# Branch B first and finished beside the gates, which go branch by branch and are summed in DRAM: one encoder layer on one Trainium2 core

## The chip, the core and the metric

The kernel runs on one core of one Trainium2 chip. A core has a matrix engine (TensorE, PE), a vector engine (VectorE, DVE), a scalar engine (ScalarE, ACT), a general engine (GpSimd, POOL) and SyncE (SP), which here only starts transfers. The metric is the device time of one execution in microseconds (us). Before the change it is 1698.8 us, the median of three runs (1694.76, 1698.8 and 1701.2).

## What is computed

One layer of a hybrid encoder on 1024 prompt tokens and 32 sample tokens, with a model width of 1024, five branches of width 256, and a feed-forward block. All of it is in float32:

```python
xn = rmsnorm(x, norm1_g)
z = xn @ w_in
ga = jax.nn.gelu(za)
va = layernorm(ga[..., W:], a_ln_g, a_ln_b)
oa = ua * gmlp_spatial(va, a_ws, a_bs)
b_in = zb[..., :W] * jax.nn.sigmoid(zb[..., W:])
b_ext = jnp.concatenate([hist_b, b_in], axis=1)
ob = jax.nn.silu(layernorm(causal_dwconv(b_ext, b_conv_w) + b_conv_b, b_ln_g, b_ln_b))
c_ext = jnp.concatenate([hist_c, c_c * c_x], axis=1)
oc = c_b * causal_dwconv(c_ext, c_conv_w)
od = multiscale_pool(d_ext, pos0, d_w, d_scale)
oe = memory_attention(zq, mem_k, mem_v)
branches = (oa, ob, oc, od, oe)
...
    merged = merged + jax.nn.sigmoid(xn @ w_gate[n] + b_gate[n]) * (branches[n] @ w_branch[n])
x = x + merged @ w_out
x = x + (jax.nn.silu(hn @ w_ffn_gate) * (hn @ w_ffn_up)) @ w_ffn_down
```

`z` is cut into two parts for A, two for B, three for C, one for D and one, the query, for E. Convolution B has 31 taps, C has 3. The states of B, C and D, the memory's keys and values, and the normalised rows of A are outputs too.

## The kernel before

Channels lie on the 128 partitions and tokens along the free axis. The 1056 tokens are two halves (`c` = 0, 1) of 528 columns, each of two quarters of 264 (256 prompt and 8 sample tokens). Each float32 factor is split in a high and a low part (`split`, L141: a copy on ACT, L148, and a subtraction on DVE, L149), and a product takes three passes (`product`, L166). A projection `z` is 128 output channels of one half: 8 input blocks x 3 passes x 2 quarters, 48 matmuls. Its result lies in a pair of PSUM banks. There are two such pairs and four single banks in the first pool of PSUM (`ps1`). When attention is done, `banks.close()` ends it, and a second one with two single banks and three pairs (`ps2`) begins.

Work is put in program order by hand. A `runner` holds a generator, and calling it with a number runs that many of its yields, so that pieces of attention (`att_bg`), of convolution B (`b_bg`) or of the rescaling of the tokens (`again`) stand between two products. Each engine then executes its own instructions in the order in which they stand, and waits where an input is not there.

The order is: memory keys and values; the query `q`; branch C on `xn`, which is x times the norm's weight, with the row factors `r1` and their squares applied behind the product (`x_factor`, `x_spread`); the tokens loaded again and multiplied by `r1`, which gives `xs` (`rescale`); branch B on `xs`, with attention two steps to a projection; D's projection with attention and convolution B beside it; A's projections `ua` and `va` with Gelu, and the rest of convolution B; then the branch products (`branch`) in the order E, C, A, D, B, with D's pooling alone in front of its product. Each product of 128 channels and one half takes 12 matmuls, is copied by ACT (`pb`, L1012) and written to DRAM by a DMA that POOL issues (`pb_d`, L1013).

Convolution B (`conv_b`, L726 to L737) is 60 multiply-and-add instructions (L733) and two plain ones over all 1086 columns of `b_ext` into a second buffer `b_y`, followed by the norm in four pieces (`norm_b`).

The gates are 20 steps, `steps = [(p, n) for p in range(KT // 2) for n in BRANCHES]`, each a pair of output blocks of one branch, computed by seven products of half size (`ORDER`: a11, a12, s2, s1, s3, s4, a22), 24 matmuls a unit. DVE and ACT make the sums and splits of the weights (L1090, L1148, L149) and gather the results (L1179 to L1199). `merge` (L1159 to L1169) takes the sigmoid, multiplies by the branch product (`pin`) and adds to `acc`, which stays in SBUF over the five branches of a pair and is then written to `mg_d`. `load_pair` brings the raw weights of the next step, two tiles, into three buffers.

## Time and profile before

| what | value |
|---|---|
| median of three runs | 1698.8 us |
| the profiled execution | 1698.78 us |
| its span, first to last instruction | 1696.9 us |
| granted clock of PE, mean | 0.987 |
| ACT busy, POOL busy | 686.9 us, 109.6 us |

The profiled execution is the median one, and 1.9 us lie outside its span. Busy times say how much of the span an engine worked. The windows divide the span, and give for each stretch the busy time of every engine beside the clock that PE was granted (1.00 is full speed, 2.4 GHz). A timeline's row is a run of like instructions, and the bracket at its end tells how long the engine sat idle before it, and what ended that. Groups by line give the mean duration of one instruction.

### The profile page before, as it was taken

The page shows a single profiled execution, that of the slowest core. Times are in us where ns is not written, and L with a number is a line of the kernel's source. Part 1 is how long each engine was busy: PE and PEld are TensorE (multiplying, and loading weights), DVE is VectorE, ACT ScalarE, POOL GpSimd, SP SyncE. Part 2 cuts the span into 40 slices and gives each one's busy share as a digit, 9 for nine tenths or more (in the row PEclk, how much of TensorE's full clock was granted, in tenths as well). Part 3 has the DMA queues.
Part 4 walks back from the last instruction along what each step waited for, and adds up shares of the span by engine and source line. Part 5 has one row for each costly group of instructions (what it writes and reads, how often), then busy time and mean ns, then how long its engine had stood idle before and what let it go on. Part 6 is the DMA issues. An engine that isn't in the chain of part 4 may idle for free.

```text
span 1696.9 us, 31557 instructions
## 1 busy us (share of the span) xinstructions
PE 1647.5 (97%) x13248; PEld 1623.0 (96%) x13248; DVE 1107.6 (65%) x1900; ACT 686.9 (40%) x1273; POOL 109.6 (6%) x217
## 2 busy tenths in 40 slices
PE   9999979899999999999999999999999999999997
PEld 8998959889999999999999999999999999999997
DVE  7678998774566677676666786666666666242345
ACT  6325752575544444444452343333333334131221
POOL 0020000223300000000000000000000003000000
PEclk9999979999999999999999999999999999999999
DMA  8252100446723334234362112222222228231012
GB/s 296 84 182 75 39 14 26 156 153 233 277 76 102 127 102 156 86 103 140 120 263 86 64 64 77 87 77 76 76 76 76 76 89 330 101 115 47 29 38 103
DMA packets 59647, 190.87 MB, mean 112 GB/s; under 512 B 9168, under 2 KB 12816, under 8 KB 59504
## 3 DMA queue, kind: packets, MB, share of 16 engines
q1 hardware_dynamic: 35328, 112.75, 20.7%
q0 software_dynamic: 20624, 73.72, 11.7%
q10 hardware_dynamic: 3552, 2.37, 0.4%
...
## 4 chain that ended last, share of the span: by engine, by line
PE 85%; DVE 5%; issue 4%; DMA 2%; ACT 2%; POOL 2%; SPq 0%; POOLq 0%; DVEq 0%; ACTq 0%
PE sa L166 28%; PE sy L166 14%; PE dn L166 13%; PE z L166 7%; PE sx L166 7%; PE wo L166 5%; PE pb L166 2%; PE dq L166 2%; PE va L166 2%; DVE b_y L733 1%; POOL pb_d L1013 1%; PE fs L320 1%; PE ov L166 1%; PE fu L166 1%; DMA pb_d<-pb 1%
## 5 line engine op out<-in xcount | busy, mean ns | idle before, releaser
L166 PE MATMUL sa<-x,s 128*128 128x264 f32 x1968 | 252.6, 284 | 0.0
L166 PEld LDWEIGHTS sa<-x,s 128*128 128x128 f32 x1968 | 244.9, 188 | 0.0
L166 PE MATMUL dn<-hp,hl 128*128 128x264 f32 x1824 | 222.2, 284 | 0.0
L166 PEld LDWEIGHTS dn<-hp,hl 128*128 128x128 f32 x1824 | 222.1, 188 | 0.1
L149 DVE TENSOR_TENSOR s<-s,s 128x512 fp32r<-128x512 f32 x164 | 112.9, 689 | 89.1 <-ACT s L148 88.1
L148 ACT ACTIVATE hl<-raw 128x512 fp32r<-128x512 f32 (+1 forms) x132 | 79.3, 616 | 214.6 <-PE dn L166 125.1
L148 ACT ACTIVATE s<-s 128x512 fp32r<-128x512 f32 x164 | 103.3, 631 | 153.4 <-PE sa L166 77.6
L149 DVE TENSOR_TENSOR hl<-raw,hl 128x512 fp32r<-128x512 f32 (+1 forms) x132 | 87.2, 673 | 89.1 <-ACT hl L148 88.8
L166 PE MATMUL sy<-x,s 128*128 128x264 f32 x984 | 126.2, 284 | 0.0
L166 PE MATMUL sa<-t,a 128*128 128x264 f32 x984 | 125.9, 284 | 0.0
L166 PEld LDWEIGHTS sy<-x,s 128*128 128x128 f32 x984 | 122.2, 188 | 0.0
L166 PEld LDWEIGHTS sa<-t,a 128*128 128x128 f32 x984 | 122.0, 188 | 0.0
L149 DVE TENSOR_TENSOR a<-fr,a 128x512 fp32r<-128x512 f32 x123 | 85.0, 691 | 52.7 <-ACT a L148 52.5
L166 PE MATMUL z<-xs,hl 128*128 128x264 f32 x768 | 99.2, 289 | 9.4 <-DVE oc L687 3.5
L148 ACT ACTIVATE a<-fr 128x512 fp32r<-128x512 f32 x123 | 78.0, 634 | 72.8 <-issue 67.0
L166 PEld LDWEIGHTS z<-xs,hl 128*128 128x128 f32 x768 | 97.1, 193 | 10.6 <-issue 5.7
L166 PE MATMUL z<-xn,hl 128*128 128x264 f32 x768 | 94.4, 284 | 1.8 <-ACT r L378 1.8
L166 PEld LDWEIGHTS z<-xn,hl 128*128 128x128 f32 x768 | 93.5, 188 | 2.3 <-ACT r L378 2.1
L166 PE MATMUL wo<-mg,hl 128*128 128x264 f32 x768 | 94.2, 284 | 0.0
L166 PEld LDWEIGHTS wo<-mg,hl 128*128 128x128 f32 x768 | 93.4, 188 | 0.2
L166 PE MATMUL pb<-br,hl 128*128 128x264 f32 x576 | 76.8, 294 | 6.3 <-ACT br L148 5.0
L1421 DVE TENSOR_TENSOR y<-y,dn 128x528 f32<-128x528 f32 x40 | 28.0, 703 | 82.4 <-PE dn L166 82.4
...
## 6 DMA issues: line engine op xcount, KB each, us to landing
pb_d<-pb POOLq DMA_DIRECT2D x80, 264.0 KB, 2.8
...
```

What stands on the lines that cost most here:

```text
L148: nc.scalar.activation(hl[:, 0], src, AF.Copy)
L149: nc.vector.tensor_tensor(hl[:, 1], src, hl[:, 0].bitcast(F32), op=ALU.subtract)
L166: nc.tensor.matmul(out, w(wi), rhs, start=start and i == 0, stop=stop and i == n - 1, skip_group_check=not (start and stop),)
L320: nc.tensor.matmul(ps[:, q, t0 : t0 + n], ones[: rows[i]], diag[: rows[i], q * Q + t0 : q * Q + t0 + n], start=True, stop=True,)
L733: nc.vector.scalar_tensor_tensor(b_y[:, j, :LB], b_ext[:, j, k : k + LB], col("bw", 31 * j + k), b_y[:, j, :LB], op0=ALU.mult, op1=ALU.add,)
L1013: nc.gpsimd.dma_start(pb_d[n][mt][:, c], out)
L1421: nc.vector.tensor_tensor(quarters(dst), quarters(dst), ps, op=ALU.subtract)
```

## The change

Branch B comes first, on `xn`. The squares of x are put beside the query's products, with the factors of the first half (`x_factor`, `x_spread`) between the last of them. B's projections are multiplied by `r1` behind PSUM, and `xs` is made beside them. C follows on `xs`, with its first tap on ACT. Attention now runs one step to a projection, from C to the last tile of A's `va`. D's projection comes behind A, after the change of PSUM pools.

Convolution B is done per channel half and in pieces of 512, 512 and 32 columns: the first tap on ACT, 30 on DVE, of which the last writes back into `b_ext`. It begins beside `ua` and goes on beside everything that follows, the first 16 gate steps included (`b_bg(2.5)` before each unit). There its norm is finished too, and branch 1's own products (`own_b`) are computed, in single banks and with weights in sixteen small tiles.

The gates go branch by branch, four pairs each. The first branch writes its gated product to `mg_d` by a plain DMA, the next three add to it with accumulating DMAs on POOL's queue, and the last one loads the sum (`acc`) and adds on DVE. The raw weights have two buffers in place of three, asked for behind the last use, and the merge buffers `ft` three in place of four. The FFN shares both.

```diff
-    epool = stage.enter_context(tc.tile_pool(name="epool", bufs=3))
+    epool = stage.enter_context(tc.tile_pool(name="epool", bufs=2))
...
-    for i in (16, 17, 10, 12, 11, 13, 8, 9, 6, 4, 7, 5, 14, 15, 0, 1):
+    for i in (16, 17, 6, 4, 7, 5, 10, 12, 11, 13, 8, 9, 0, 1):
         want("w_in", i)
     for i in (0, 1):
         want("w_va", i)
-    for n in BRANCHES:
+    for i in (14, 15):
+        want("w_in", i)
+    for n in BRANCHES[:-1]:
...
-        spreads[c] = factors([r1[c]], D, late=True)[1]
+        spreads[c] = factors([r1[c]], D, late=True, narrow=True)[1]
 
     def x_spread(c):
-        ps = spreads[c]()
-        nc.scalar.activation(quarters(r1q[c]), ps, AF.Square)
-        nc.scalar.copy(quarters(r1[c]), ps)
+        for q_, ps in enumerate(spreads[c]()):
+            nc.scalar.copy(r1[c][:, q_ * Q : q_ * Q + Q], ps[:, :Q])
...
+    for c in range(NC):
+        x_squares(c)
...
+            if c == 1:
+                (x_factor, x_spread)[j](0)
...
+    again = runner(rescale(0), rescale(1))
     for j in range(2):
         wb_ = [wview(slab()) for _ in range(2)]
         for c in range(NC):
-            ps = projected(wb_[0], c, xs)
-            if j == 0 and c == 0:
-                again(2)
-            elif j:
-                att_bg(2)
+            ps = projected(wb_[0], c, xn)
+            if j == c == 0:
+                x_factor(1)
+            else:
+                again()
             sb = temp(f"sb{j}_{c}")
-            nc.scalar.activation(quarters(sb), ps, AF.Sigmoid)
-            ps = projected(wb_[1], c, xs)
-            if j == 0 and c == 0:
-                again(2)
+            nc.vector.tensor_tensor(quarters(sb), ps, quarters(r1[c]), op=ALU.mult)
+            nc.scalar.activation(sb, sb, AF.Sigmoid)
+            ps = projected(wb_[1], c, xn)
+            if j == c == 0:
+                x_spread(1)
             else:
-                att_bg(2)
+                again()
+            nc.vector.tensor_tensor(sb, sb, r1[c], op=ALU.mult)
...
-        b_y = epool.tile([P, 2, EXT], F32, name="b_y", tag="ext")
         for j in range(2):
-            nc.vector.tensor_scalar(
-                b_y[:, j, :LB], b_ext[:, j, 0:LB], col("bw", 31 * j), col("bb", j), op0=ALU.mult, op1=ALU.add
-            )
-            yield
-            for k in range(1, 31):
-                nc.vector.scalar_tensor_tensor(
-                    b_y[:, j, :LB], b_ext[:, j, k : k + LB], col("bw", 31 * j + k), b_y[:, j, :LB],
-                    op0=ALU.mult, op1=ALU.add,
+            for t0, n in ((0, SEQ // 2), (SEQ // 2, SEQ // 2), (HB + SEQ, DEC)):
+                y = temp("by")[:, :n]
+
+                def tap(k):
+                    return b_ext[:, j, t0 + k : t0 + k + n]
+
+                nc.scalar.activation(
+                    y, tap(HB), AF.Identity, bias=col("bb", j), scale=col("bw", 31 * j + HB)
                 )
-                yield 0.33
-        for c in range(NC):
-            br[1][c] = [unit(F32R, f"ob{c}_{j}") for j in range(2)]
-        normed = [norm_b(b_y, i) for i in range(4)]
-        for t in range(3 * 4 + 6):
-            for i in range(4):
-                if 3 * i <= t:
-                    next(normed[i], None)
-            yield
-
-    def norm_b(b_y, i):
-        lo = i * QP
-        w = QP if i < 3 else LB - lo
-        ys = [b_y[:, j, lo : lo + w] for j in range(2)]
-        both = temp("bsm")
-        sm = both[:, :w]
+                for k in range(HB - 1, -1, -1):
+                    dst = tap(0) if k == 0 else y
+                    nc.vector.scalar_tensor_tensor(
+                        dst, tap(k), col("bw", 31 * j + k), y, op0=ALU.mult, op1=ALU.add
+                    )
+                    yield 0.7 if n > DEC else 0.1
...
+            nc.scalar.activation(y, tap(0), AF.Copy, scale=col("cw", 3 * j))
...
+                ps = projected(wc_[i], c, xs)
+                if j == c == 0:
+                    again()
+                else:
+                    att_bg()
+                evac(j, c, ps)
...
+    def own_b(c):
+        for mt in range(KT):
+            raw = fpool.tile([P, 2, P], F32, name=f"wr{c}_{mt}", tag="wr", bufs=1)
+            nc.sync.dma_start(
+                raw, a["w_branch"][2 + mt // 4].rearrange("p (k n) -> p k n", k=2)[:, :, mt % 4 * P : (mt % 4 + 1) * P]
+            )
+            w = fpool.tile([P, 2, 2, P], F32R, name=f"wp{c}_{mt}", tag="wp", bufs=2)
+            split(w, raw)
+            out = temp("pb")
             yield
-
-    b_bg = runner(conv_b())
-
+            for q_ in range(2):
+                cols = slice(q_ * Q, q_ * Q + Q)
+                ps = bank("pb")[:, :Q]
+                product(
+                    ps, [(lambda i, k=k: w[:, i, k], lambda i, k=k: br[1][c][k][:, i, cols]) for k in range(2)]
+                )
+                nc.scalar.copy(out[:, cols], ps)
+                if q_ == 1:
+                    nc.gpsimd.dma_start(pb_d[1][mt][:, c], out)
+                yield 2
+        br[1][c] = None
+
+    def whole_b():
+        yield from conv_b()
+        yield from norm_b(None)
+        for c in range(NC):
+            yield from norm_b(c)
+            yield from own_b(c)
+
+    b_bg = runner(whole_b())
...
+        project(ua_evac, xs, lambda: (att_bg(), b_bg(2)))
+        att_bg()
+        b_bg(0.7)
...
-    d_bg = runner(pool_mix())
-    d_bg.drain()
-    to_parts(3)
-    branch(3, rest((comb, 0.5)))
-    branch(1, rest((comb, 0.5)))
+    pool_bg = runner(pool_d())
+
+    def beside_c(i):
+        if i == 4:
+            to_parts(0)
+        pool_bg()
+        b_bg(0.4)
+
+    branch(2, beside_c)
+    pool_bg.drain()
+    mix_bg = runner(mix_d())
+
+    def beside_a(i):
+        if i % 2 == 1 and i < 8:
+            mix_bg()
+        elif i == 8:
+            mix_bg.drain()
+            to_parts(3)
+        elif i > 8:
+            comb(0.5)
+        if i > 3:
+            b_bg(0.4)
+
+    branch(0, beside_a)
+    branch(3, lambda i: (comb(0.5), b_bg(0.4)))
...
-            if n_raw[0] % 3 == 2:
-                r = fpool.tile([P, 1024], F32, name=f"fr{p}", tag="fraw", bufs=1)
-            else:
-                r = wpool.tile([P, 1024], F32, name=f"fr{p}", tag="raw", bufs=2)
-            n_raw[0] += 1
+            r = wpool.tile([P, 1024], F32, name=f"fr{p}", tag="raw", bufs=2)
...
-                if n == "s3":
+                if n == ORDER[-1][0]:
                     load_pair(pairs, fraws, p + 1)
...
-    steps = [(p, n) for p in range(KT // 2) for n in BRANCHES]
+    steps = [(p, n) for n in BRANCHES for p in range(KT // 2)]
...
+        pin[n, mt] = unit(F32, f"pi{mt}_{n}")
+        nc.sync.dma_start(pin[n, mt], pb_d[n][mt])
+        if n == BRANCHES[-1]:
+            acc[mt] = unit(F32, f"acc{mt}")
+            nc.gpsimd.dma_start(acc[mt], mg_d[mt])
...
+            nc.vector.tensor_tensor(g, g, pin[n, mt][:, c], op=ALU.mult)
             if n == BRANCHES[0]:
-                nc.vector.tensor_tensor(acc[mt][:, c], acc[mt][:, c], g, op=ALU.mult)
-                return
-            nc.vector.tensor_tensor(g, g, pin[n, mt][:, c], op=ALU.mult)
-            nc.vector.tensor_tensor(acc[mt][:, c], acc[mt][:, c], g, op=ALU.add)
+                nc.gpsimd.dma_start(mg_d[mt][:, c], g)
+            elif n != BRANCHES[-1]:
+                nc.gpsimd.dma_start(mg_d[mt][:, c], g, accum_op=ALU.add)
+            else:
+                nc.vector.tensor_tensor(acc[mt][:, c], acc[mt][:, c], g, op=ALU.add)
...
+        if i < 4 * KT // 2:
+            hooks = {m: lambda: b_bg(2.5) for m, _ in ORDER}
+        if i == 4 * KT // 2 - 1:
+            b_bg.drain()
```

Line numbers shift: `split` is L149 and L150 in the new kernel, convolution B's taps L674, the sums of weights L1100, the gates' gathering L1200 to L1210, `merge`'s multiplication L1174, A's Gelu L808 and L841, attention's exponential L524, its scaling L529 and its transposed copies L546.

First place: ACT in the stretch of the query's products, from the last split of `xn` on (`hl` are split weights, `sq` and `r` squares of x, `q` the copies out of PSUM). Before:

```order
L148 ACTIVATE hl_0_300<-raw_136 128x512
L148 ACTIVATE hl_1_301<-raw_136 128x512
L363 ACTIVATE sq_522<-x_1_128 128x528
L363 ACTIVATE sq_525<-x_1_128 128x528
L363 ACTIVATE sq_528<-x_2_132 128x528
L430 COPY q_298<-z 128x528
L148 ACTIVATE hl_0_310<-raw_306 128x512
L148 ACTIVATE hl_1_311<-raw_306 128x512
L430 COPY q_298<-z 128x528
```

and now:

```order
L369 ACTIVATE sq_304<-x_1_131 128x528
L369 ACTIVATE sq_307<-x_1_131 128x528
L369 ACTIVATE sq_310<-x_2_135 128x528
L149 ACTIVATE hl_0_346<-raw_139 128x512
L149 ACTIVATE hl_1_347<-raw_139 128x512
L365 ACTIVATE r_234<-x_0_129 128x528
L365 ACTIVATE r_234<-x_0_259 128x528
L149 ACTIVATE hl_0_356<-raw_352 128x512
L149 ACTIVATE hl_1_357<-raw_352 128x512
L437 COPY q_344<-z 128x528
```

The first copy of `q` stood ahead of the split of the third weight (`raw_306`) and now stands behind it, and behind three squares and two that start the row sums.

Second place: ACT beside A's `va` tiles (`va` the Gelu, `pe` attention's exponentials and scalings, `pt` its transposed copies). Before:

```order
L148 ACTIVATE hl_1_3017<-raw_2750 128x512
L884 ACTIVATE ua_2742<-z 128x528
L148 ACTIVATE hl_0_3024<-raw_2867 128x512
L884 ACTIVATE ua_2743<-z 128x528
L148 ACTIVATE hl_1_3025<-raw_2867 128x512
L917 ACTIVATE va_3011<-va 128x256 x4
L917 ACTIVATE va_3012<-va 128x256 x4
```

and now:

```order
L841 ACT_TABLE_LOAD
L841 ACTIVATE va_all<-va 128x256
L546 ACTIVATE pt_2456<-tp 128x2x128
L524 ACT_TABLE_LOAD
L524 ACTIVATE pe,sm<-sc,mx 128x256
L546 ACTIVATE pt_2458<-tp 128x2x128
L524 ACTIVATE pe,sm<-sc,mx 128x256
L841 ACT_TABLE_LOAD
L841 ACTIVATE va_all<-va 128x256
L529 ACTIVATE pe<-pe,sm 128x256 x2
```

Eight Gelus stood together, without attention; now each stands between exponentials, with a table load on either side.

Third place: DVE in a gate step (`s`, `a` sums and low parts of weights, `p` and `u` results, `pi` the branch products or the sum; `by` and `b_ext` convolution B). Before, from the first gathering of a step on:

```order
L1189 TENSOR_TENSOR p_7_6820<-sx,p_7_6820 128x528
L149 TENSOR_TENSOR a_8_6884<-fr_6784,a_8_6884 128x512
L1168 TENSOR_TENSOR p_7_6820<-p_7_6820,pi_0_6777 128x528
L1169 TENSOR_TENSOR pi_4_6320<-pi_4_6320,p_7_6820 128x528
L149 TENSOR_TENSOR a_8_6912<-fr_6784,a_8_6912 128x512
L149 TENSOR_TENSOR s_8_6945<-s_8_6943,s_8_6945 128x512
L1194 TENSOR_TENSOR p_7_6819<-sa,p_7_6819 128x528
L149 TENSOR_TENSOR s_8_6976<-s_8_6941,s_8_6976 128x512
L1090 TENSOR_TENSOR s_8_7053<-s_8_6943,fr_6784 128x512
L1168 TENSOR_TENSOR p_7_6819<-p_7_6819,pi_0_6816 128x528
L1169 TENSOR_TENSOR pi_4_6360<-pi_4_6360,p_7_6819 128x528
```

and now, in step 1:

```order
L1200 TENSOR_TENSOR p_1_5051<-sx,p_1_5051 128x528
L150 TENSOR_TENSOR s_1_5056<-s_1_5054,s_1_5056 128x512
L674 SCALAR_TENSOR_TENSOR by<-b_ext,vec,by 128x512
L150 TENSOR_TENSOR a_1_5088<-fr_4836,a_1_5088 128x512
L674 SCALAR_TENSOR_TENSOR by<-b_ext,vec,by 128x512
L1174 TENSOR_TENSOR p_1_5051<-p_1_5051,pi_4_5003 128x528
L674 SCALAR_TENSOR_TENSOR by<-b_ext,vec,by 128x512
L150 TENSOR_TENSOR a_2_5126<-fr_5091,a_2_5126 128x512
L674 SCALAR_TENSOR_TENSOR by<-b_ext,vec,by 128x512
L150 TENSOR_TENSOR a_2_5158<-fr_5091,a_2_5158 128x512
```

The additions to the sum (L1169) are gone from there, and a tap of 512 columns stands behind nearly every instruction. Between the first gatherings of steps 0 and 3 stand 44 wide and 30 narrow taps.

## Rows read from the trace of the kernel before

**Rows 1.** The head of the page and its busy times by engine (share, instructions).

```profile
span 1696.9 us, 31557 instructions
PE 1647.5 (97%) x13248; PEld 1623.0 (96%) x13248; DVE 1107.6 (65%) x1900; ACT 686.9 (40%) x1273; POOL 109.6 (6%) x217
```

**Rows 2.** The table by windows: start:end, length, busy us of each engine (instructions), granted clock, DMA.

```profile
75.00:450.00 375.00, 340.31 (x2569) 322.20 (x2568) 288.20 (x543) 196.71 (x444) 60.01 (x113) 0.95 0.35 117
225.00:250.00 25.00, 15.55 (x66) 9.47 (x67) 21.44 (x41) 12.23 (x39) 0.00 (x0) 0.57 0.00 0
325.00:350.00 25.00, 19.61 (x141) 18.88 (x140) 14.77 (x47) 18.96 (x33) 5.14 (x12) 0.86 0.36 130
350.00:375.00 25.00, 21.86 (x157) 20.91 (x158) 20.74 (x54) 20.59 (x45) 6.58 (x13) 0.93 0.36 134
450.00:863.00 413.00, 413.00 (x3414) 413.00 (x3413) 284.56 (x430) 185.18 (x301) 9.61 (x18) 1.00 0.39 126
```

**Rows 3.** PE's timeline at two holes: start, length, instruction, idle before and releaser.

```profile
227.26 1.11 PE L530 MATMUL tp<-ident,pe 128*128 128x128 f32 x4 [3.52 <-ACT pe L523]
...
337.11 1.40 PE L166 MATMUL pb<-br,hl 128*128 128x264 f32 x3 [4.99 <-ACT br L148]
```

**Rows 4.** The table by windows of 2 us, behind the first hole.

```profile
224.00:226.00 2.00, 0.00 (x0) 0.00 (x0) 2.00 (x5) 1.29 (x5) 0.00 (x0) 0.81 0.00 0
...
236.00:238.00 2.00, 2.00 (x7) 0.98 (x6) 0.87 (x3) 0.59 (x1) 0.00 (x0) 0.50 0.00 0
```

**Rows 5.** Groups by line and shape, 75 to 457 us: busy, mean ns; idle and releasers.

```profile
L733 DVE SCALAR_TENSOR_TENSOR b_y<-b_ext,vec,b_y 128x1086 f32<-128x1086 f32 x60 | 80.7, 1345 | 0.8
```

**Rows 6.** Groups by line and shape, 75 to 457 us: convolution C's taps.

```profile
L644 DVE SCALAR_TENSOR_TENSOR oc<-c_ext,vec,oc 128x512 f32<-128x512 f32 x8 | 6.0, 746 | 0.0
...
L644 DVE SCALAR_TENSOR_TENSOR oc<-c_ext,vec,oc 128x16 f32<-128x16 f32 x8 | 1.8, 229 | 0.0
```

**Rows 7.** Timeline of the first projections, PE's row and ACT's.

```profile
19.73 40.97 PE L166 MATMUL z<-xn,hl 128*128 128x264 f32 x336
...
33.91 1.16 ACT L148 ACTIVATE hl<-raw 128x512 fp32r<-128x512 f32 x2 [6.10 <-DMA raw<-in_w_in]
...
35.45 0.63 ACT L148 ACTIVATE hl<-raw 128x512 fp32r<-128x512 f32 x1
```

**Rows 8.** Groups by line and shape on ACT, 75 to 457 us.

```profile
L518 ACT ACTIVATE pe<-sc,mx 128x256 f32<-128x256 f32 x32 | 14.8, 469 | 4.3 <-DVE mx L516 4.2
...
L523 ACT ACTIVATE pe<-pe,sm 128x256 f32<-128x256 f32 x32 | 14.5, 503 | 3.3 <-DVE sm L521 3.3
...
L540 ACT ACTIVATE pt<-tp 128x256 fp32r<-128x256 f32 x32 | 12.1, 380 | 2.9 <-PE tp L530 1.5 <-DVE pt L541 1.3
...
L518 ACT ACTIVATION_READ_ACCUMULATOR pe<-sc,mx 128x1 f32 x32 | 6.4, 199 | 0.0
...
L773 ACT ACT_TABLE_LOAD x4 | 5.1, 1283 | 0.3 <-DVE b_y L771 0.2
...
L917 ACT ACTIVATE va<-va 128x256 f32<-128x256 f32 x8 | 3.1, 384 | 18.8 <-PE va L166 18.8
```

**Rows 9.** Groups by line and shape on PE, 75 to 457 us.

```profile
L166 PE MATMUL va<-hl,xs 128*128 128x256 f32 x192 | 22.8, 280 | 0.0
...
L512 PE MATMUL sc<-ks,qs 128*128 128x256 f32 x64 | 11.9, 302 | 0.5 <-DVE e L547 0.5
...
L530 PE MATMUL tp<-ident,pe 128*128 128x128 f32 x64 | 11.3, 296 | 4.5 <-ACT pe L523 4.5
```

**Rows 10.** PE's timeline, the first unit of gate steps 0 and 1.

```profile
456.80 3.06 PE L166 MATMUL sa<-xs,a 128*128 128x264 f32 x24
...
477.14 3.06 PE L166 MATMUL sa<-xs,a 128*128 128x264 f32 x24
```

**Rows 11.** Groups by line and shape, 457 to 864 us: the gates' additions to the sum.

```profile
L1169 DVE TENSOR_TENSOR pi<-pi,p 128x528 f32<-128x528 f32 x47 | 33.2, 706 | 1.0
```

**Rows 12.** DMA issues on the page: KB each, us from issue to landing.

```profile
pb_d<-pb POOLq DMA_DIRECT2D x80, 264.0 KB, 2.8
```

391 lines of the change are left out of this document (174 added, 217 removed).

## The prediction

> **What bounds the kernel now.** I read the page's busy times first. TensorE (PE) is busy 1647.5 of 1696.9 us, VectorE (DVE) 1107.6 [rows 1]: with the same matmuls, the time can fall only where PE waits or runs slowly. So the second view is the table by windows [rows 2]. The row of 75 to 450 us, from the first input projections to the last branch products, has 340.31 us of PE busy in 375: 34.7 us of idle. From 450 to 863, the gates, PE is busy all of 413 us at clock 1.00. The change rewrites the first stretch, and hangs new work on the second. Idle is not the whole price. The clock is 0.57 in 225 to 250, 0.86 in 325 to 350, 0.93 in 350 to 375 [rows 2]; times the busy PE of each row, at full clock these would have taken 15.55 x 0.43 + 19.61 x 0.14 + 21.86 x 0.07 = 11.0 us less. So 45.7 us is the most that a better order of this stretch gives.
>
> The PE timeline shows two of the holes: 3.52 us before attention's transpose, and 4.99 us before the product that follows pool D [rows 3]. In windows of 2 us the clock falls to 0.50 (the lower of 1.2 and 2.4 GHz) behind the first hole, is still there at 236 to 238 us [rows 4], so some 13 us, and costs half of that, 6.5 us, besides the hole. Both holes are chains through ScalarE (ACT) and DVE. DVE explains the first: branch B's convolution, 60 instructions of 1345 ns, 80.7 us [rows 5], runs between attention's reductions, and DVE is busy 21.44 of 25 us there [rows 2].
>
> **The change, part by part.**
>
> *Convolution B.* The 60 instructions of 1345 ns go [rows 5]. In their place, for 2 channel halves and two token halves, stand 120 taps of 512 columns, and 60 taps of 32. The nearest rows are convolution C's: 746 ns for 512, 229 ns for 16 columns [rows 6]. 120 x 0.746 + 60 x 0.229 = 103.3 us, which is 22.6 more than the 80.7. By the order, 44 wide and 30 narrow ones of them run in the gates: 32.8 + 6.9 = 39.7 us. Before the gates DVE thus holds 63.6 us of taps in place of 80.7, spread from the projections of A to the last products. Attention, spread one step to a projection, no longer competes with them until A. So neither hole has its old cause, and I count the 45.7 us as gained and take the new waits off one by one.
>
> *The start.* Seven projections take 40.97 us without a gap, 5.85 each [rows 7]. Two PSUM pairs hold them, so the third waits for the first's copy. Before, ACT copies the first, then waits 6.10 us for a weight, until 33.91 [rows 7]. In the new order the weight's split stands ahead of the first copy (front section, ACT). The copy comes at about 35.1 (33.91 + 1.16), its pair frees at 35.7. The second projection ends at 19.73 + 2 x 5.85 = 31.4, or 1.1 later, since three squares of the size of a split (1.16/2 us each [rows 7]) now precede its weight and take 1.7 us, 0.6 of which ACT sat idle: 32.5. So PE waits some 3.2 us. The column sums of the squares now stand between the third and fourth projection and need DVE's seven additions, which in the order stand among 13 instructions of some 0.65 us behind 35.2 us: about 44 us, against a third projection that ends at 41.5. Together with its start, 6 to 8 us are lost. With a little slow clock I take 9; bounds 3 (the weight comes earlier) and 15 (clock at half for 13 us).
>
> *Tables.* Attention's exponentials now alternate with A's Gelu. By the order, A's two stages hold 23 table loads where 1 stood: 22 x 1283 ns [rows 8] = 28.2 us more on ACT. For a tile of va ACT has two loads, one Gelu, two exponentials with their accumulator reads, two scalings and two transposed copies: 2.57 + 0.38 + 1.34 + 1.01 + 0.76 = 6.06 us [rows 8]. PE has 192/8 = 24 matmuls of va, 22.8/8 = 2.85, a step's transposes 11.3/16 and scores 11.9/16 [rows 9]: 4.30. The excess is 1.76 a tile, 15.8 for nine. ACT's instructions overlap by 0.1 each (two splits take 1.16, one 0.63 [rows 7]), eleven a tile, which leaves 0.66 a tile, 5.9. I take 8, nearer to the overlapped figure; bounds 0 and 28.2. The ua stage, with 5.85 of projection beside it, I cost at nothing.
>
> *B on xn, C on xs, the pools' move.* The same matmuls; B's evacuation gains two DVE multiplications by the row factors a tile, C's loses its own, and the change of PSUM pools comes behind A. No row shows these waits. B and C are 20 projections, 117 us; at the old rate of idle (34.7 in 375 us) that is 10.8. I take 4, since DVE has no large taps there any more; bounds 0 and 11.
>
> *Products.* Branch 1's 192 matmuls move into the gates, which costs PE nothing. Pool D runs beside the products in place of a drained PE, so the 4.99 us hole goes; in its place the copies of products (ACT) and taps compete. I take 4; bounds 0 and 10 (the idle of 325 to 375, 5.39 + 3.14 [rows 2], and some clock).
>
> *Gates.* DVE is busy 284.56 us in 413 [rows 2], with steps of 20.34 us [rows 10]: 14.0 a step. Merging by DMA takes 48 additions of 706 ns out [rows 11], and the first branch never had one, so with some 11.8 a step the first three steps hold 35.4 + 39.7 of taps + about 3 of the norm = 78 us, against 61.0 of PE. DVE falls 17 us behind. What it may lag before PE feels it is the three PSUM pairs, two to three units of 20.34/7 = 2.9 us, about 8. So PE loses 9. Bounds: 0, if the weights prepared ahead cover all, and 25.6: each instruction that the order lists in these steps at its full duration, chained, sums to 86.6, and no lag. The own products wait on this chain, nobody on them until step 16.
>
> *Accumulating DMAs.* 48 of 264 KB, four a step. No row has one; a plain one lands in 2.8 us [rows 12], and reading the target and writing it may take three times that, 8.4: 4 x 8.4 = 33.6 against 20.34 if they run singly. A merge buffer (two of three a step) is written again some 15 us later, so I take nothing; bounds 0 and the 13 us a step of the singly running case. Raw weights with two buffers in place of three, in gates and FFN, I cost at nothing: DVE's 6 us of slack in a step of 20.34 cover a load asked for late (a 264 KB one lands in 2.8 us [rows 12], so 3 to 6 for 512 KB, an estimate), and without that slack a step would be as much longer.
>
> **Sum.** 45.7 - 9 - 8 - 4 - 4 - 9 = 11.7 us. The profiled run took 1698.78 with a span of 1696.9, and is the median shown, 1698.8. Forecast 1698.8 - 11.7 = **1687**.
>
> **Rivals.**
>
> *A, the waits hide.* Weights and PSUM cover the gates' taps (9 us), ACT's overlap covers the tables (8), the start loses 5 rather than 9: 1687 - 21 = **1666**. For it: PE's queue was full all through the gates with DVE at 14.0 of 20.34. Against it: DVE's sum in three steps is above PE's, whichever durations are taken.
>
> *B, tables set the pace of A.* All 22 loads lie on PE's path, since the transposes of a step wait for the scalings behind the loads: 28.2 in place of 8: **1707**. The transposes waited 3.52 us for a scaling in the old order too [rows 3]. Against it: scores and transposes of another step stand between. The Trainium skill (ScalarE: Activation LUTs, section Table sets: the hidden batching unit) says to batch activations by table set, which speaks against this part of the change, and budgets about 2.7 us for a switch. This trace has 1.283 us for a load; by the page's budget the 22 switches would be 59 us, an estimate, and this rival would stand at 1738. The measured row decides.
>
> *C, slower: taps make DVE the bound in the gates.* Place: steps 0 to 3. No lag is left, since the sums that free PSUM stand behind chained taps on the same engine: 25.6 us lost, and if two holes reach 3.5 us, as the one in [rows 3], the clock halves twice for 13 us [rows 4], 13 more. 25.6 + 13 - 9 = 29.6: **1717**. It decides once single waits pass 3.5 us; taps of 0.746 in chains of four to five in the order make holes of that size possible, but not certain.
>
> *D, the change does not do what it says about DMAs*: accumulations run singly and the merges wait, 13 us for each of 12 steps: **1843**. One queue that carries 264 KB in 2.8 us speaks against it.
>
> **How the numbers follow.** Chances: forecast 0.40, A 0.20, B 0.16, C 0.20, D 0.04. About 0.5%, 8.5 us, can be told from no change, so faster means below 1690.3 and slower above 1707.3. The forecast's own bounds put two thirds of it below 1690.3, the rest within. Faster: 0.27 + 0.20 + 0.03 of B = 0.50. Same: 0.12 + 0.09 + 0.04 of C = 0.25. Slower: 0.01 + 0.04 + 0.16 + 0.04 = 0.25. The range runs from A to C, 1664 to 1717, with D and the tails outside; the forecast's own is 1675 to 1699.
>
> **What would show it.** Right: idle in 0 to 75 us of 5 to 10, no hole of 3 us before the product that follows pool D, ACT nearly full from ua to va with waits of transposes on scalings, PE idle of 5 to 15 in the first four gate steps and none behind. Wrong: clock below 0.9 in the gates (C), gate steps over 21 us behind the fourth with waits on merge buffers (D), a va stage no slower than 4.4 us a tile (A), or idle between 75 and 450 still above 30 us.

## The result and the profile after

The changed kernel takes 1714.5 us (median of four runs, 1713.5 to 1715.9). The ratio to the kernel before is 1.0094, 95% interval 1.0072 to 1.0115, so it is slower by about 0.9%. The forecast was 1687, faster; the time lies inside the range (1664 to 1717), near the number of rival C.

The head of its page, and the busy times by engine, as in [rows 1]:

```profile
span 1714.1 us, 32020 instructions
PE 1654.2 (97%) x13246; PEld 1629.3 (95%) x13246; DVE 1081.3 (63%) x1946; ACT 717.4 (42%) x1324; POOL 164.2 (10%) x289
```

PE's idle has grown from 49.4 (1696.9 - 1647.5) to 59.9 us (1714.1 - 1654.2). The other 7 us of the 17 are busy time: the same matmuls ran at a lower mean granted clock, 0.985 against 0.987. The table by windows shows where, with the columns of [rows 2]:

```profile
25.00:50.00 25.00, 19.90 (x151) 19.66 (x150) 22.36 (x48) 12.57 (x22) 0.00 (x0) 0.86 0.51 172
75.00:200.00 125.00, 124.84 (x1020) 123.39 (x1019) 71.78 (x144) 63.30 (x138) 8.47 (x15) 1.00 0.28 82
200.00:275.00 75.00, 60.46 (x422) 52.53 (x421) 55.35 (x135) 65.97 (x162) 0.00 (x0) 0.91 0.09 29
300.00:450.00 150.00, 139.00 (x1057) 135.38 (x1057) 123.66 (x221) 71.65 (x126) 41.53 (x77) 0.97 0.60 206
450.00:525.00 75.00, 64.01 (x490) 61.13 (x490) 66.54 (x150) 36.21 (x64) 6.49 (x12) 0.93 0.30 99
850.00:900.00 50.00, 45.72 (x357) 44.87 (x356) 34.12 (x54) 24.43 (x42) 6.55 (x13) 0.97 0.77 291
```

And the same stretches of the kernel before:

```profile
25.00:50.00 25.00, 25.00 (x208) 25.00 (x208) 22.95 (x39) 15.30 (x29) 0.00 (x0) 1.00 0.61 208
75.00:200.00 125.00, 116.49 (x933) 113.04 (x932) 106.39 (x189) 63.46 (x136) 14.86 (x26) 1.00 0.31 96
200.00:275.00 75.00, 62.87 (x423) 53.72 (x422) 68.54 (x104) 38.50 (x132) 0.00 (x0) 0.84 0.08 23
300.00:450.00 150.00, 135.96 (x1005) 130.66 (x1004) 93.27 (x215) 88.89 (x164) 45.15 (x87) 0.95 0.57 198
450.00:525.00 75.00, 75.00 (x622) 75.00 (x622) 47.93 (x72) 33.92 (x56) 3.24 (x6) 1.00 0.42 135
850.00:900.00 50.00, 50.00 (x414) 49.70 (x413) 32.96 (x68) 23.62 (x42) 2.96 (x8) 1.00 0.59 225
```

I add to each stretch's idle the time that its slow windows of 25 us cost (busy x (1 - clock)), as the prediction did:

| stretch of the changed kernel | idle | slow clock | sum | term of the forecast |
|---|---|---|---|---|
| 25 to 50, the query | 5.1 | 2.8 | 7.9 | 9 |
| 75 to 200, B, C and the first ua | 0.2 | 0 | 0.2 | 4 |
| 200 to 275, end of ua, va, end of attention | 14.5 | 5.4 | 20.0 | 8 |
| 300 to 450, products, first gate step | 11.0 | 4.4 | 15.4 | 4 |
| 450 to 525, gate steps 1 to 3 | 11.0 | 3.9 | 14.9 | 9 |
| 850 to 900, last gate step, w_out | 4.3 | 1.7 | 6.0 | 0 |
| sum | 46.1 | 18.2 | 64.4 | 34 |

The same sum over the windows of 75 to 450 us of the kernel before is 34.67 + 13.65 = 48.3. In that stretch the changed kernel loses 35.6 us (0.2 + 20.0 + 15.4), which is 12.7 less. At the start and in the gates it loses 28.8 us (7.9 + 14.9 + 6.0), where the rows of the kernel before are full at clock 1.00. 28.8 - 12.7 is 16.1, against a span that is 17.2 longer. So what decided is the size of the new losses. In the chain of work that ended last PE has 62% of the span, 85% before; 13 of the 23 points went to "issue", which the profile puts down to no engine.

What PE waited for, longest sums first (engine, line, releaser: us, times, longest):

```profile
PE pb L167 <- ACT pb L1021: 8.9, 7, 2.9
PE fs L326 <- DVE diag L313: 5.8, 2, 4.0
PE sa L167 <- DVE p L1205: 5.3, 4, 1.9
PE z L167 <- ACT q L437: 5.1, 1, 5.1
PE lm L688 <- DVE bsm L685: 2.7, 1, 2.7
PE tp L536 <- ACT va_all L841: 2.7, 1, 2.7
```

They name the products on ACT's copies, the norm's small matmuls `fs` and `lm` in the gates on DVE, the gates' results `sa` (3.2 of the 5.3 us lie at 850 to 900), the query's copy at the start, and transposes on ACT in the va stage. The first of them stood in the kernel before too, and was smaller:

```profile
PE pb L166 <- ACT pb L1012: 3.7, 5, 1.7
```

### The profile page after: what moved, and what is told of

The parts are those of the page before. It is cut to its first block, busy times and chain, and to the rows that moved or that the text cites. A ratio compares the mean times of both kernels' runs of the same rounds, so it can differ in the third digit from the quotient of the medians.

```text
span 1714.1 us, 32020 instructions
## 1 busy us (share of the span) xinstructions
PE 1654.2 (97%) x13246; PEld 1629.3 (95%) x13246; DVE 1081.3 (63%) x1946; ACT 717.4 (42%) x1324; POOL 164.2 (10%) x289
## 3 DMA queue, kind: packets, MB, share of 16 engines
q0 software_dynamic: 29968, 95.35, 18.2%
## 4 chain that ended last, share of the span: by engine, by line
PE 62%; issue 17%; DVE 8%; DMA 5%; ACT 4%; POOL 3%; POOLq 0%; SPq 0%; DVEq 0%; ACTq 0%
PE sa L167 19%; PE dn L167 13%; PE sy L167 9%; PE z L167 8%; PE sx L167 5%; DVE by L674 3%; PE pb L167 2%; PE dq L167 2%; PE wo L167 1%; POOL pb_d L1022 1%; POOL mg_d L1178 1%; DMA mg_d<-acc 1%; PE fs L326 1%; ACT L524 1%; DMA mr<-mg_d 1%
## 5 line engine op out<-in xcount | busy, mean ns | idle before, releaser
L149 ACT ACTIVATE s<-s 128x512 fp32r<-128x512 f32 x164 | 102.9, 631 | 157.6 <-PE sy L167 63.4
L149 ACT ACTIVATE hl<-raw 128x512 fp32r<-128x512 f32 (+1 forms) x128 | 76.7, 614 | 197.3 <-PE dn L167 124.6
L150 DVE TENSOR_TENSOR hl<-raw,hl 128x512 fp32r<-128x512 f32 (+1 forms) x128 | 84.6, 671 | 81.9 <-ACT hl L149 81.5
L150 DVE TENSOR_TENSOR a<-fr,a 128x512 fp32r<-128x512 f32 x123 | 84.9, 690 | 78.2 <-ACT a L149 78.0
L150 DVE TENSOR_TENSOR s<-s,s 128x512 fp32r<-128x512 f32 x164 | 113.1, 690 | 32.8 <-ACT s L149 32.0
L167 PE MATMUL z<-xs,hl 128*128 128x264 f32 x960 | 121.9, 288 | 1.7 <-DVE e L553 1.7
L167 PEld LDWEIGHTS z<-xs,hl 128*128 128x128 f32 x960 | 120.1, 192 | 1.9 <-issue 1.8
L149 ACT ACTIVATE a<-fr 128x512 fp32r<-128x512 f32 x123 | 77.4, 632 | 64.6 <-issue 53.2
L674 DVE SCALAR_TENSOR_TENSOR by<-b_ext,vec,by 128x512 f32<-128x512 f32 (+1 forms) x174 | 99.7, 588 | 1.9 <-ACT by L669 0.5
L167 PEld LDWEIGHTS pb<-br,hl 128*128 128x128 f32 x576 | 74.6, 199 | 8.6 <-ACT pb L1021 8.6
```

Of the source, the lines that this page charges most:

```text
L149: nc.scalar.activation(hl[:, 0], src, AF.Copy)
L150: nc.vector.tensor_tensor(hl[:, 1], src, hl[:, 0].bitcast(F32), op=ALU.subtract)
L167: nc.tensor.matmul(out, w(wi), rhs, start=start and i == 0, stop=stop and i == n - 1, skip_group_check=not (start and stop),)
L674: nc.vector.scalar_tensor_tensor(dst, tap(k), col("bw", 31 * j + k), y, op0=ALU.mult, op1=ALU.add)
```

## The experiments

Theory: the time is the sum of five separate losses. (1) Table loads make ACT the bound of A's stage, (2) the burst of taps puts DVE behind PE in the gates, (3) the last branch's turn of loading and writing the sum delays the end of the gates, (4) the start waits for copies and for the first factor, (5) products wait for a free tile or a held ACT. The main rival to each is that the wait only moves. The first four edits were made on the changed kernel alone, the later ones on top of other edits, as each section says. Ratios are to the kernel before.

### Tables away: e1_no_tables

```diff
-            nc.scalar.activation(quarters(br[0][c][:, j]), ps, AF.Gelu_apprx_tanh)
+            nc.scalar.activation(quarters(br[0][c][:, j]), ps, AF.Copy)
...
-        nc.scalar.activation(va[i][:n], ps, AF.Gelu_apprx_tanh)
+        nc.scalar.activation(va[i][:n], ps, AF.Copy)
```

> The Gelu of ua and va is replaced by a plain copy, so that part of branch A's computation is left out, and with it the table loads of ACT in these two stages (23 in the order) go; nothing is moved. Theory 1 (table loads make ACT the bound of the va tiles: 5.4 us a tile on ACT against 4.3 on PE): PE's idle in 200 to 275 us falls from 14.5 us to under 5, the clock stays at 1.00 there, and the time falls by 14 to 19 us, to 1696 to 1701. Rival (attention's chain between DVE and ACT, one step to a tile, sets the pace, and the loads are hidden beside it): the idle stays above 9 us and the time falls by less than 6.

Measured: 1702.2 us, ratio 1.0020 [1.0007, 1.0032], 12 us less than the changed kernel, a little short of the 14 to 19 expected. The A stage in its windows:

```profile
200.00:275.00 75.00, 71.37 (x559) 65.18 (x559) 55.77 (x141) 44.86 (x149) 0.00 (x0) 1.00 0.10 31
```

Idle is 3.6 us in place of 14.5, and the clock 1.00 in place of 0.91: the stage gives 16.3 us back. ACT falls from 65.97 to 44.86 us. The copies take as long as the Gelus did (0.37 us a `va` tile against 0.38), so it is the loads and what they hold up that went. In the changed kernel ACT's timeline has the period of a tile, from one Gelu (`va_all`) to the next:

```profile
224.28 1.28 ACT L841 ACT_TABLE_LOAD   x1
225.57 0.38 ACT L841 ACTIVATE va_all<-va 128x256 f32<-128x256 f32 x1
...
227.04 1.28 ACT L524 ACT_TABLE_LOAD   x1
...
229.65 1.28 ACT L841 ACT_TABLE_LOAD   x1
230.94 0.39 ACT L841 ACTIVATE va_all<-va 128x256 f32<-128x256 f32 x1
```

The period is 230.94 - 225.57 = 5.37 us, with two loads of 1.28 in it; five of the seven steps between full tiles take 5.33 to 5.38. That is theory 1; the rival (under 6 us) falls. The whole gained 12 us where the stage gave 16; where the other four went is open.

### A slower rate in the gates: e2_rate_1_3

```diff
-            hooks = {m: lambda: b_bg(2.5) for m, _ in ORDER}
+            hooks = {m: lambda: b_bg(1.3) for m, _ in ORDER}
```

> Convolution B's rest, its norm and its products are spread over the 16 gate steps at 1.3 in place of 2.5 units of work a product. Theory 2 (a burst of taps puts DVE behind PE in gate steps 0 to 3, and the norm's small products, which stand in PE's queue, wait for the late DVE): 14 taps a step fit beside the gates, PE's idle of 10.1 us in 475 to 500 falls below 3, the clock stays at 1.00, and the time falls by 10 to 15 us, to 1700 to 1705. Rival (the norm's chain of DVE, ACT and PE blocks PE for its own length wherever it stands): holes of 3 to 4 us before lm and fs come again in later steps, and the time falls by less than 6.

Measured: 1705.3 us, ratio 1.0039 [1.0023, 1.0055], 9 us less. Gate steps 1 to 3:

```profile
450.00:525.00 75.00, 72.96 (x595) 72.23 (x593) 67.93 (x130) 30.60 (x53) 8.96 (x15) 1.00 0.46 140
```

Idle is 2.0 us in place of 11.0, at clock 1.00, as theory 2 says; the total of 9 us is just short of the 10 to 15 expected. The changed kernel's timeline shows what the late DVE did to PE: the largest holes stand before the norm's matmuls, which lie in PE's queue between the gates' units.

```profile
480.83 3.35 PE L167 MATMUL sa<-xs,a 128*128 128x264 f32 x24 [1.30 <-DVE p L1200]
...
488.54 3.15 PE L167 MATMUL sx<-xs,a 128*128 128x264 f32 x24 [1.42 <-DVE u L1210]
...
494.44 0.64 PE L688 MATMUL lm<-bsm,ones 128*128 128x32 f32 x2 [2.75 <-DVE bsm L685]
...
495.96 0.27 PE L289 MATMUL fm<-ones,bsm 128*32 128x1 f32 x2 [0.89 <-DVE bsm L694]
...
500.25 0.63 PE L326 MATMUL fs<-diag,ones 32*128 32x32 f32 x2 [4.02 <-DVE diag L313]
```

Of the 11.0 us of idle 7.7 stand before the norm's three matmuls (2.75 + 0.89 + 4.02), and 3.3 before the gates' own units (1.30, 1.42, and 0.59 at 459 us). With 14 wide taps a step in place of 18 and 26, one hole of 1.35 us is left before `lm`, so the chain does not cost its own length wherever it stands.

### Another queue for the sum's loads: e3_acc_on_sp

```diff
-            nc.gpsimd.dma_start(acc[mt], mg_d[mt])
+            nc.sync.dma_start(acc[mt], mg_d[mt])
```

> The last branch's loads of the sum are issued by SyncE in place of GpSimd. Theory 3 (GpSimd's queue is in order: a load of the next sum stands behind the write of the last one, which waits for VectorE, so it lands late and the additions and the weights behind them are late): PE's waits of 1.3 to 1.9 us in the last two gate steps go, and the time falls by 3 to 6 us, to 1708 to 1711. Rival (the loads are bound by the transfers themselves, 6.7 us each at a busy time): within 2 us of the changed kernel.

Measured: 1722.2 us, ratio 1.0145 [1.0123, 1.0167]: slower than the changed kernel, which neither said. The end of the gates lost more:

```profile
850.00:900.00 50.00, 43.55 (x330) 42.87 (x329) 33.01 (x52) 22.91 (x39) 5.33 (x10) 0.93 0.75 281
```

6.5 us idle and clock 0.93, against 4.3 and 0.97, which makes 3.4 of the 8 us that the whole lost; the rest is open. Theory 3 in this form falls: the place in GpSimd's queue is not what makes the loads late. In SyncE's queue they stand among the weights and branch products; whether that is the extra loss was not tried.

### Squares later: e4_squares_late

```diff
-    for c in range(NC):
-        x_squares(c)
...
-            if c == 1:
-                (x_factor, x_spread)[j](0)
+            if c == 0:
+                x_squares(j)
+            elif j == 1:
+                x_factor(0)
...
             if j == c == 0:
+                x_spread(0)
                 x_factor(1)
```

> The squares of x stand behind the first two products of the query again, and the factor of the first half behind the fourth one. Theory 4 (the first copy of q stands behind a weight's split that waits for a transfer): the 5.1 us hole before the third projection goes, the clock stays at 1.00 in 25 to 50 us, and the time falls by 5 to 8 us, to 1706 to 1709. Rival (the wait moves to branch B's first results, which need the row factors): the hole comes back behind 45 us, and the time falls by less than 3.

Measured: 1722.0 us, ratio 1.0141 [1.0123, 1.0159], 7 us more than the changed kernel in place of a gain. The hole before the third projection went, and a new one came 17 us later, before the spread of the first factor:

```profile
25.00:50.00 25.00, 24.60 (x201) 24.07 (x199) 21.45 (x39) 13.62 (x26) 0.00 (x0) 1.00 0.63 216
50.00:75.00 25.00, 22.41 (x148) 21.99 (x149) 19.65 (x52) 12.64 (x26) 5.47 (x9) 0.80 0.48 164
```

```profile
43.55 6.10 PE L167 MATMUL z<-xn,hl 128*128 128x264 f32 x48
52.59 3.02 PE L326 MATMUL fs<-diag,ones 128*128 128x128 f32 x12 [2.94 <-DVE diag L313]
```

2.6 us of idle and a clock of 0.80 in 50 to 75 cost what 25 to 50 gave back. The rival is right on the wait: by the trace DVE made additions of the squares until 47.9 us, among them the second half's, and turned to the first half's factor only then. That the kernel as a whole was some 7 us slower than the changed one is not explained by this stretch, and stays open.

### Attention drained before A: e5_att_before_a

On top of the rate of 1.3.

```diff
-                    att_bg()
+                    att_bg(2)
                 evac(j, c, ps)
...
-        project(gated, xs, att_bg)
+        project(gated, xs, lambda: att_bg(2))
+
+    att_bg.drain()
...
-        project(ua_evac, xs, lambda: (att_bg(), b_bg(2)))
+        project(ua_evac, xs, lambda: b_bg(2))
...
-        att_bg()
         b_bg(0.7)
```

> On top of the slower rate of 1.3: attention runs two steps to a projection beside C and the gated products, and is drained before ua, so that no exponential stands between Gelus (2 loads in A in place of 23); nothing is left out. Theory 1 (table loads): idle and slow clock of the A stage, 20 us in the changed kernel, fall below 5, and C, which has no large taps beside it, keeps PE busy: 1690 to 1694. Rival (two steps to a projection make attention's chain the bound in C, as before the change): 8 us or more of idle come up in 130 to 200 us, and the time is 1700 or more.

Measured: 1686.5 us, ratio 0.9928 [0.9907, 0.9949], 19 us less than with the slower rate alone, and better than the 1690 to 1694 expected.

```profile
75.00:200.00 125.00, 122.91 (x970) 117.29 (x968) 79.20 (x174) 72.94 (x187) 8.46 (x15) 1.00 0.25 78
200.00:275.00 75.00, 75.00 (x606) 71.62 (x605) 50.67 (x111) 30.89 (x98) 0.00 (x0) 1.00 0.13 41
```

PE is busy all of the stretch that lost 20 us, and the stretch of C, with two steps of attention to a projection, loses 2.1. The rival falls. That is more than the tables alone gave in the first experiment, which kept 3.6 us of idle in the A stage; here none is left, as attention itself is gone from it.

### One load of the sum: e6_one_sum_load

On top of the last one.

```diff
-        if n == BRANCHES[-1]:
+        if n == BRANCHES[-1] and p == KT // 2 - 1:
             acc[mt] = unit(F32, f"acc{mt}")
...
-            elif n != BRANCHES[-1]:
+            elif n != BRANCHES[-1] or p < KT // 2 - 1:
                 nc.gpsimd.dma_start(mg_d[mt][:, c], g, accum_op=ALU.add)
...
-            if n == BRANCHES[-1] and p < KT // 2 - 1:
-                nc.gpsimd.dma_start(mg_d[mt], acc.pop(mt))
```

> On top of the last one: the last branch adds to the sum by accumulating transfers too, but for its last pair, which alone loads the sum and adds on VectorE. Theory 3b (only four tile units are free in the gates, so each pair of the last branch waits for the write of one sum, 6.3 us, before it can load the next, 6.7 us, and additions, weights and w_out behind them come late): PE's 4 to 6 us of idle and slow clock in 850 to 900 go, and the time falls by 4 to 6 us from the last one's. Rival (the queue of weight transfers with two buffers is what is late): within 2 us of it.

Measured: 1678.1 us, ratio 0.9872 [0.9852, 0.9893], 8 us less, more than the 4 to 6 expected. The end of the gates before and after this edit:

```profile
825.00:900.00 75.00, 70.62 (x573) 69.46 (x572) 50.07 (x98) 33.74 (x57) 9.26 (x19) 1.00 0.60 221
```

```profile
825.00:900.00 75.00, 73.34 (x600) 72.56 (x599) 50.64 (x99) 33.09 (x58) 8.79 (x18) 1.00 0.57 198
```

4.4 us of idle become 1.7, so 2.7 us of the 8 are gained at the end of the gates. Some 3 more lie at 500 to 525 us (idle of 2.5 at clock 0.93, then 1.1 at 1.00), where nothing was edited; the rest is not located. In the changed kernel the turn is seen on GpSimd's queue and on DVE:

```profile
844.47 0.53 POOL L1161 DMA_DIRECT2D acc<-mg_d  x1 [6.01 <-DMA mg_d<-acc]
858.11 0.53 POOL L1186 DMA_DIRECT2D mg_d<-acc  x1 [13.10 <-DVE acc L1180]
```

```profile
866.45 0.71 DVE L1180 TENSOR_TENSOR acc<-acc,p 128x528 f32<-128x528 f32 x1 [2.86 <-DMA acc<-mg_d]
```

The load of a sum waits 6.0 us for the write of the last one to land, the next write 13.1 us for DVE's addition to that sum, and an addition at 866 waited 2.9 us for its load. With accumulating transfers there is no such turn. Theory 3b holds for the place; but the edit also takes 12 of the 16 additions to the sum from DVE, and what those alone are worth was not tried.

### The products: e7_products_freed, e9_by_in_psum, e10_own_weights_late

Two edits on top of the last kernel: both (e7), the first alone (e9), the second alone (e10).

```diff
-                y = temp("by")[:, :n]
+                y = (temp("by") if psum[1] == 4 else bank("by"))[:, :n]
...
             raw = fpool.tile([P, 2, P], F32, name=f"wr{c}_{mt}", tag="wr", bufs=1)
+            if mt == 0:
+                nc.vector.tensor_copy(raw[:, 0, 0:1], br[1][c][1][:, 0, 0:1].bitcast(F32))
```

> On top of the last one: the convolution's running sums lie in a single PSUM bank once attention is done, so that the branch products have all four temporary tiles, and the first own weight of branch B is loaded only when the branch is normed. Theory 5 (products wait for a free temporary tile, since a convolution piece holds one or two of four, and once for ScalarE, which is held by a split whose transfer is late): PE's idle of 9 us in 375 to 425 falls below 3, the clock stays at 1.00, and the time falls by 8 to 12 us from the last one's. Rival (ScalarE's copies and splits themselves set the pace of the products): it falls by less than 4.

> The kernel with one sum load, plus the first half of the products' change alone: the convolution's running sums lie in a PSUM bank, the own weights are loaded as early as before. Theory 5a (the products wait for a free temporary tile): most of the idle in 375 to 425 us goes, 5 us of 7, and the time falls by 4 to 6 us, to 1672 to 1674. Rival 5b (ScalarE is held by the early split of an own weight): it falls by less than 2.

> The kernel with one sum load, plus the second half alone: the first own weight of branch B is loaded when the branch is normed, the running sums stay in temporary tiles. Theory 5a (temporary tiles): waits of 1 to 2.3 us of products on copies stay, and the time falls by less than 2 us. Rival 5b (the held ScalarE): the idle falls below 3 us and the time by 4 to 6.

Measured: both 1672.2 us, 0.9839 [0.9818, 0.9860], 6 us less where 8 to 12 were expected; the running sums in PSUM alone 1667.2, 0.9816 [0.9795, 0.9837], 11 less where 4 to 6 were expected; the late weights alone 1685.1, 0.9922 [0.9907, 0.9938], 7 more where a fall of under 2 was expected. The products' stretch, in the kernel without the edits, then with the first, then with the second:

```profile
300.00:425.00 125.00, 112.89 (x878) 109.74 (x877) 100.22 (x180) 64.18 (x113) 36.24 (x68) 0.99 0.62 214
```

```profile
300.00:425.00 125.00, 121.81 (x978) 120.20 (x977) 114.25 (x201) 69.53 (x121) 37.35 (x69) 1.00 0.68 235
```

```profile
300.00:425.00 125.00, 115.98 (x905) 113.07 (x904) 102.65 (x182) 65.36 (x114) 36.27 (x67) 0.99 0.64 220
```

12.1 us of idle become 3.2 with the sums in PSUM, and 9.0 with the late weights. So it is mainly the temporary tiles (5a). The taps themselves are no faster in PSUM (0.747 us against 0.744). A tile of a product is free only when its transfer has landed. ACT's copies waited for that, in these windows of the kernel without the edits and then with the first:

```profile
ACT pb L1022 <- DMA pb_d<-pb: 30.1, 17, 3.4
```

```profile
ACT pb L1022 <- DMA pb_d<-pb: 11.1, 9, 2.7
```

And in the changed kernel:

```profile
392.76 0.60 ACT L1021 COPY pb<-pb 128x528 f32<-128x528 f32 x1 [2.87 <-DMA pb_d<-pb]
...
400.91 1.27 ACT L1021 COPY pb<-pb 128x528 f32<-128x528 f32 x2 [3.51 <-DMA pb_d<-pb]
```

Holding the weights back did harm: later, where the branch's own products stand in the gates, idle rose from 1.2 us to 5.5, and 3.7 of it were waits of these products for the split of a weight.

```profile
500.00:700.00 200.00, 194.46 (x1556) 192.09 (x1557) 125.49 (x233) 100.42 (x178) 36.03 (x48) 0.98 0.63 151
```

ACT did wait 5.3 us for such a weight in the changed kernel, until 381 us, and a 2.9 us hole of PE ends there. In the kernel of this experiment the same wait is only 2.0 us long. So 5b falls for that kernel, while for the one hole in the changed kernel it was not tried.

### The start: e8_start, e11_start_and_own, e13_start_and_psum

e8 (on e7) has the first factor behind the third product of the query. e11 and e13 move the second half further back: its squares and the memory's sums stand behind branch B's first product. e11 has late weights, each loaded one product ahead; e13 is e9 with the start's edit alone, and here is that edit's core:

```diff
-    for c in range(NC):
-        x_squares(c)
...
-            if c == 1:
-                (x_factor, x_spread)[j](0)
+            if c == j == 0:
+                x_squares(0)
+            elif c == j == 1:
+                x_factor(0)
...
             if j == c == 0:
-                x_factor(1)
+                x_spread(0)
+                x_squares(1)
+                xu.clear()
             else:
+                if j == 0:
+                    x_spread(1)
                 again()
...
             if j == c == 0:
-                x_spread(1)
+                x_factor(1)
+                kv, vhl = memory_values()
```

> On top of the last one: the squares of the first half stand behind the first product of the query, the factor behind the third, and the squares of the second half behind the fourth. Theory 4b (the chain of sums, square root and diagonal needs to start early, and the copies of q must not stand behind a late split): 5 to 7 us of idle and slow clock in 0 to 75 us go, and the time falls by 4 to 7 us from the last one's. Rival (the first result of branch B waits for its factor wherever the squares stand): it falls by less than 2.

> The kernel with both halves, plus two edits in other places: at the start the squares of the second half, its factor and the memory's sums stand behind branch B's first product, so that the chain of the first factor has VectorE and ScalarE for itself; and each own weight of branch B is loaded and split one product ahead. Theory 4c (the start's hole is this chain, 9 us from the last addition to the diagonal, which one product of 5.9 us and a half hides if nothing else stands in it): idle and slow clock in 0 to 75 us fall from 8.4 to 4 us or less, the 5 us of idle in 525 to 700 to below 2, and the time by 5 to 8 us, to 1664 to 1667. Rival (the chain is longer than the product it hides behind wherever it stands): the hole comes back at 50 to 60 us, and the time falls by 2 to 3 for the own weights alone.

> The kernel with the running sums in PSUM and early own weights, plus the start's edit alone: the squares of the second half, its factor and the memory's sums behind branch B's first product. Theory 4c (the start's hole is the chain of the first factor and its queue, and nothing behind it takes the gain back): idle and slow clock in 25 to 50 us, 7.6 in the kernel without it, go, none comes up in 50 to 200, and the time falls by 5 to 8 us from 1667, to 1659 to 1662. Rival (the hole only moved, as the waits of 700 to 850 us in the run with both edits suggest): it falls by less than 3.

Measured: e8 1679.5 us, 0.9880 [0.9858, 0.9902], 7 us more than e7: 5.2 us of idle stood at 25 to 50 us, 4.4 in e7, now ahead of the column sums; the rest of the 7 is not explained. e11 1666.5, 0.9809 [0.9791, 0.9828]. e13 1662.6, 0.9783 [0.9766, 0.9800].

The first row is of e11, the others of e13.

```profile
700.00:850.00 150.00, 143.90 (x1164) 142.91 (x1163) 83.86 (x129) 65.26 (x115) 26.50 (x37) 0.99 0.70 193
```

```profile
25.00:75.00 50.00, 50.00 (x414) 49.65 (x413) 45.26 (x100) 31.04 (x59) 3.96 (x7) 1.00 0.58 192
75.00:200.00 125.00, 123.76 (x960) 115.76 (x958) 82.51 (x184) 78.99 (x207) 10.05 (x18) 1.00 0.27 83
525.00:850.00 325.00, 322.81 (x2632) 321.38 (x2631) 191.50 (x307) 150.52 (x269) 59.01 (x81) 0.99 0.70 181
```

With the second half out of the way PE has no idle in 25 to 75 us in either, and no hole comes up right behind it (1.2 us in 75 to 200). In e11 6.1 us were lost at 700 to 850, which e13 does not have to that size (2.2 in 525 to 850). e13 is 4.6 us faster than e9 by medians, with intervals that just overlap, where the stretch gave 7.6; theory 4c is right on the place, and a little short on the gain.

### Accumulating or plain transfers: e12_plain_dma, e14_plain_dma_psum

e12 is e7, e14 is e9, each with:

```diff
-                nc.gpsimd.dma_start(mg_d[mt][:, c], g, accum_op=ALU.add)
+                nc.gpsimd.dma_start(mg_d[mt][:, c], g)
```

> The kernel with both halves, with plain transfers in place of the accumulating ones in the gates, so that the sum over branches is left out (only the last writer of each tile and the last pair's additions remain). Theory D0 (accumulation runs beside the products and costs nothing): within 3 us of the kernel with both halves, 1669 to 1675. Rival D (accumulating transfers hold merge buffers or the memory): 8 us faster or more.

> The kernel with the running sums in PSUM and early own weights, with plain transfers in place of the accumulating ones, so that the sum over branches is left out (the last writer of each tile and the last pair's additions remain). Theory D0 (accumulation is hidden): within 3 us of 1667. Rival D2 (accumulation costs some us, which the run with late own weights showed as waits of own products): 4 to 7 us faster.

Measured: e12 1666.0 us, 0.9806 [0.9790, 0.9822], 6 us less than e7; e14 1664.2, 0.9793 [0.9774, 0.9813], 3 us less than e9 with intervals that overlap. Theory D0 holds for e14, at the edge of its 3 us. The 6 us of e12 lie between D0 and its rival D: there the own products' waits for the split of a late weight fell from 4.2 to 1.2 us with the plain transfers; that the two kinds of transfer compete is not shown. The landing of the products' plain transfers in the changed kernel, and then of the 48 accumulating ones, by their line (the page's row of `mg_d<-p` mixes 36 of them with 12 plain ones):

```profile
pb_d<-pb POOLq DMA_DIRECT2D x80, 264.0 KB, 3.6
```

```profile
L1178 POOL DMA_DIRECT2D mg_d<-p x36: 846/859/897, 536.3 to 794.4; - x36
...
DMA to landing us min/median/max: 3.9/5.2/7.9
```

## Why the prediction was wrong

**What goes away.** Right in part. The step "So neither hole has its old cause" held: the largest hole before a product is 2.9 us now, and without the table loads (e1) the stretch of attention's end keeps 3.6 us of idle, with taps of convolution B still beside it. But "I count the 45.7 us as gained" took in waits that the old order shares with the new one, such as the products' waits for ACT's copies, 3.7 us before and 8.9 now. By place, 75 to 450 us lost 48.3 us and now loses 35.6, a gain of 12.7; the prediction's terms made it 29.7 (45.7 - 8 - 4 - 4).

**The sum of new waits** is what failed: 34 us forecast, 64.4 measured. Mechanisms and places were mostly named; three terms (tables, products, gates) were of the wrong size, one (the end of the gates) was left out, and a part common to all, the clock, was missing.

1. *Tables*, 8 forecast, 20.0 measured. The period on ACT came out as computed: 5.37 us, between the overlapped figure (4.96) and the full one (6.06), so 1.07 a tile over PE's 4.30 and 9.6 for nine tiles. The step "I take 8" left out what stands around the tiles: the idle was 14.5. The trace has attention's waits and the copies of `xd` on ACT ahead of the first Gelu there; their shares were not separated. It left out the slow clock too, 5.4. e1 shows that 16.3 of the 20.0 hang on the loads. Rival B had the mechanism; its 28.2 was too much. The Trainium skill (ScalarE: Activation LUTs, section Table sets: the hidden batching unit) says to batch activations by set, which speaks against this part of the change. The runs agree: keeping attention apart from the Gelus gained 19 us in e5. By the Trainium skill's figure of about 2.7 us a switch, 22 loads would have been 59 us, an estimate; a load was 1.28 us in this trace too.
2. *Products*, 4 forecast, 15.4 measured. The step "copies of products (ACT) and taps compete" had the wrong resource. The four temporary tiles are shared by products and convolution pieces, and a tile is held until its transfer lands, 3.6 us after the change against 2.8 [rows 12]. e9 shows it: with the sums elsewhere, 8.9 us of idle went, and ACT's waits for landings fell from 30.1 to 11.1 us.
3. *Gates*, 9 forecast, 14.9 measured. DVE's lag was right (it is busy 66.5 of 75 us there). The prediction charged PE with what the lag exceeds PSUM's slack, 9 us, and only 3.3 us stood before the gates' own units there (1.6 more in the step before). Its step "nobody on them until step 16" overlooked that the norm's matmuls stand in PE's own queue, so that PE waits for DVE's chain itself: 7.7 us, 4.0 of it in one hole. The slow clock added 3.9. That 9 is near 11.0 of idle is luck.
4. *The end of the gates*, 0 forecast, 6.0 measured. No step spoke of the last branch's loads of the sum at all: a write of a 528 KB tile that the next load waits for. PE waited there for DVE's results and for parts of the sum (`sa` 3.2, `wo` 1.1 us). e6 points to the turn of loads, with 2.7 us gained in that place, but lightens DVE as well; e3 shows only that the queue of the loads was not it.
5. *The start*, 9 forecast, 7.9 measured, and half of the stated mechanism: a 5.1 us hole before the third projection, on the copy of `q`, where about 3 had been worked out, then slow clock. The second hole, of some 2.5 us at the column sums (44 against 41.5), did not come. So the size is in part luck.
6. *B and C*, 4 forecast, 0.2 measured.
7. *The clock.* The kernel before had 11 to 14 us of slow clock in 35 us of idle, and the prediction counted that as gained. It put no such share on its own new holes but in one term. They cost 18.2 on 46.1 us of idle. The same share on the 34 us forecast would have made 47, an estimate, and a time of 1700: no change. Rival C charged the clock only for holes of 3.5 us; the rows do not bear this out, since the clock was 0.86 and 0.93 in the two windows of 375 to 425 us, where PE's longest wait was 2.9.

Rival C was near in time mostly for other reasons than its own: its sign showed, a clock below 0.9 in the gates (0.87 in 475 to 500 us), but their first steps lost 14.9, not 38.6. Rival D falls by e14. Of the prediction's signs of being right, idle of 5 to 10 us in 0 to 75 (7.0) and of 5 to 15 in the first gate steps came; "none behind" did not, with 4.3 us at 850 to 900.
